# A hybrid decoder step: decode products in five heads, mixed rows loaded one group ahead, weighted rows turned in the last quarter

## Chip, core and metric

The kernel runs on one core of a Trainium2 chip. The metric is device time in microseconds. Before the change three runs gave 1744.0, 1746.33 and 1751.34 us, median 1746.33.

## The reference

One step of a hybrid decoder layer for a prompt of T = 1024 tokens and eight sample tokens, side by side as NT = 1032 columns, at model width 1024, in f32:

```python
h = rmsnorm(x, norm1_w)
q_r, f_r, i_r, g_r, z, xbc_r, dt_r = split(h @ w_in)
o_a = rmsnorm(hgrn2(silu(q_r), 1 - f, i_r, log(f)), hgrn_norm_w) * silu(g_r)      # 8 heads of 128
y   = rmsnorm((ssd(conv(xbc_r), dt) + D * X) * silu(z), ssm_norm_w)               # 16 heads of 64
x   = x + concat(o_a, y) @ w_out                                                   # 2048 -> 1024
gate, val = split(rmsnorm(x, norm2_w) @ w_up)                                      # 2 x 2816
x   = x + (silu(conv3(gate)) * val) @ w_down
y_out = rmsnorm(x, final_norm_w)
```

The prompt starts from zero states; the sample tokens update given states (one 128 x 128 matrix for each HGRN head and token, one 64 x 128 matrix for each SSM head and token), which are outputs too.

## The kernel before

Activations lie transposed: features on the 128 partitions, the 1032 columns along the free axis. Every large product is three f32r products, a high and a low part of each factor without low times low (`hh,wh`, `hl,wh`, `hh,wl`). ACT casts the high part (`split` and `split_in`, L199 and L1135), DVE subtracts for the low part (L201, L1136).

The input projection is a list of jobs of 128 output rows each (`z`, `xbc`, then `f q v sg` for each head). A stream of recurrence work is woven into it: `drive` runs a generator that yields weights, and after each yield lets PE do the share of matmul steps of the jobs that the weight stands for. `after(n, work)` runs work n steps later; `spread` runs the pieces of a generator n steps apart. So the order on every engine follows from the program's order and the yields.

The eight HGRN heads run in this weave, some 62 us each, beside the jobs of the next head. `head(h, t)` makes the values `vt`, decays `tt` and the intra-chunk products `a` in levels: `f`, `q`, `k`, `v` are scaled by `tt` (L980, L981, copies L983, L984), then short matmuls fill `a` at 128*64, 128*32 and 128*16. Then come the sample tokens' product `od` (from the states `Sh`, loaded by SP, updated by DVE at L959 and POOL at L958 and L960), the products `kv`, the running state `SS` (L1072, L1074), and the output `o`, normed and gated into `sg`. The head's `rstd` goes by DRAM (`hr_d`) to a broadcast `sq`; `scale_out` multiplies `sg` by it (L1121) and stores it as a row of `mix_d`, the mixed rows, from which the output projection reads.

The SSM decode has eight steps (two groups g, four steps i). `ssm_decode` runs in the z jobs, `decode_beside` beside a head: `load` (L690 to L693: state `Sd`, rows `Bb` and `Cb`), `front` (DVE `Bb`, ACT scaling of `Sd`, DVE sum, store, POOL products) and `back` (DVE reductions, L710, L711). Before, z jobs hold steps 0 and 1 of group 0, and heads 1 to 6 hold one step each. `load` is issued behind the state's store of the same head, `front` behind `od`'s copy, `back` behind the copy of its turned rows (L1081). Behind the last step of a group come `decode_gate` and, 80 steps later, `decode_norm` (L735 to L737, L730), which stores the sample columns of four mixed rows (L731). Rows 12 to 15 are complete only behind the second norm, which before stands in head 7.

The output projection runs in groups of four mixed rows. `mix_load(r0)` loads, casts and splits rows 8 to 11 beside head 6's end, and rows 12 to 15 beside head 7. The first group's results are copied out of PSUM by ACT (L1177).

SP issues nearly all DMAs, in order: one that waits holds up those behind it. Weights (`ws`) are loaded two jobs ahead.

At the end the down projection's last two groups of rows run by quarters of the columns, in the order 3, 0, 1, 2. For each quarter eight results are added to `x` (L1567), and each 128 columns are transposed (`fin`, L1574), squared and summed by ACT (L1576), rooted, and scaled by `rstd` and the final norm's weights (`fw`), then stored (L1588).

## Time and profile before

| what | us |
|---|---|
| median of three runs | 1746.33 |
| the profiled execution | 1747.35 |
| its span in the trace | 1745.6 |
| busy: PE, DVE, ACT, POOL | 1704.6, 1094.0, 782.0, 487.7 |

The trace has every instruction's start and duration; times are from the span's start. A row of the timeline has the start, the duration, engine, line, operation, the tiles out<-in, the shape, and in brackets how long the engine stood idle before it and what ended that. "issue" there means that the profile shows nothing that the engine waited for. `SPq` rows are the DMAs that SP issues. A window's DMA line gives the busy share of the 16 DMA engines in tenths, in 40 equal slices; `q8 instruction` are packets of instructions that are being fetched.

### The profile page before, as it was taken

What the parts mean: (1) busy time and instruction counts of PE and PEld (TensorE: products, weight loads), DVE (VectorE), ACT (ScalarE), POOL (GpSimd) and SP (SyncE); (2) the same over time, 40 slices, a digit from 0 to 9 for tenths busy, and PEclk for the clock granted to TensorE, in tenths of its full rate; (3) what the DMA queues carried; (4) which work ended last, traced back from release to release, by engine and by line L of the source; (5) the groups of instructions that cost most, each with busy time, mean ns of one, the idle gap of its engine ahead of it and who ended that gap; (6) DMA issues with size and microseconds to landing.
All of it is one profiled execution on the core that took longest, in us unless ns stands there. A gap on an engine that the chain in (4) does not pass through costs nothing. (4 is left out here: it accounts for less than half of the span.)

```text
span 1745.6 us, 38507 instructions
## 1 busy us (share of the span) xinstructions
PE 1704.6 (98%) x16119; PEld 1657.3 (95%) x16119; DVE 1094.0 (63%) x1979; ACT 782.0 (45%) x1427; POOL 487.7 (28%) x501
## 2 busy tenths in 40 slices
PE   7999999999999999999999989999999999999998
PEld 7999999899989999999999989999999999999997
DVE  6668666555754655567746688666767667444545
ACT  7677685344445444445333464333334434111114
POOL 2102131110210211111122266666666664000002
PEclk9999999999999999999999999999999999999999
DMA  5354334533442443345437722222222226422212
GB/s 165 73 123 123 92 91 146 157 90 101 137 127 64 137 123 99 112 141 155 138 125 244 239 81 78 82 96 74 74 73 81 79 97 214 154 71 79 94 61 98
DMA packets 250036, 200.22 MB, mean 115 GB/s; under 512 B 47972, under 2 KB 221526, under 8 KB 249846
## 3 DMA queue, kind: packets, MB, share of 16 engines
q1 hardware_dynamic: 249574, 197.67, 37.4%
q8 instruction: 126, 2.06, 0.5%
q14 instruction: 48, 0.39, 0.1%
q0 software_dynamic: 288, 0.10, 0.0%
HBM read 155.16 MB, written 46.95 MB: 116 GB/s over the span
## 5 line engine op out<-in xcount | busy, mean ns | idle before, releaser
L93 PE MATMUL mm<-hl,wh 128*128 128x344 f32 x1248 | 405.2, 325 | 0.0
L93 PE MATMUL mm<-hh,wh 128*128 128x344 f32 x1248 | 404.9, 325 | 0.0
L93 PE MATMUL mm<-hh,wl 128*128 128x344 f32 x1248 | 402.0, 322 | 0.0
L93 PEld LDWEIGHTS mm<-hl,wh 128*128 128x128 f32 x1248 | 235.3, 189 | 4.8 <-issue 4.1
L93 PEld LDWEIGHTS mm<-hh,wh 128*128 128x128 f32 x1248 | 235.3, 189 | 4.0 <-issue 3.4
L93 PEld LDWEIGHTS mm<-hh,wl 128*128 128x128 f32 x1248 | 235.4, 189 | 1.4 <-issue 1.2
L199 ACT CAST wh<-ws 128x1024 fp32r<-128x1024 f32 x96 | 100.6, 1048 | 260.7 <-PE dn L93 134.8
L93 PE MATMUL ub<-uh,wh 128*128 128x258 f32 x704 | 200.1, 284 | 3.8 <-DVE fext L1432 2.7
L93 PE MATMUL ub<-ul,wh 128*128 128x258 f32 x704 | 199.5, 283 | 0.0
L93 PE MATMUL ub<-uh,wl 128*128 128x258 f32 x704 | 199.4, 283 | 0.0
L93 PE MATMUL dn<-ah,wh 128*128 128x256 f32 (+1 forms) x640 | 181.2, 283 | 2.0 <-DVE x L1549 2.0
L93 PE MATMUL dn<-al,wh 128*128 128x256 f32 (+1 forms) x640 | 180.6, 282 | 0.0
L93 PE MATMUL dn<-ah,wl 128*128 128x256 f32 (+1 forms) x640 | 180.1, 281 | 0.0
L201 DVE TENSOR_TENSOR wl<-ws,wh 128x1024 fp32r<-128x1024 f32 x88 | 109.7, 1247 | 93.3 <-ACT wh L199 92.6
L93 PE MATMUL mm<-mh,wh 128*128 128x258 f32 x512 | 146.5, 286 | 4.1 <-DVE x L1179 4.0
L93 PE MATMUL ua<-uh,wh 128*128 128x258 f32 x528 | 149.5, 283 | 0.8 <-DVE val L1444 0.4
L93 PE MATMUL ua<-ul,wh 128*128 128x258 f32 x528 | 149.2, 282 | 0.0
L93 PE MATMUL ua<-uh,wl 128*128 128x258 f32 x528 | 148.4, 281 | 0.0
L93 PE MATMUL mm<-ml,wh 128*128 128x258 f32 x512 | 145.3, 284 | 0.6 <-DVE ml L1136 0.6
L93 PE MATMUL mm<-mh,wl 128*128 128x258 f32 x512 | 144.9, 283 | 0.0
L93 PEld LDWEIGHTS ub<-uh,wh 128*128 128x128 f32 x704 | 133.6, 190 | 4.4 <-DVE fext L1432 2.9
L1382 DVE TENSOR_TENSOR wl<-wt,wh 128x512 fp32r<-128x512 f32 x88 | 89.4, 1035 | 74.2 <-ACT wh L1381 74.2
(373 smaller groups left out, 3987.4 us busy)
## 6 DMA issues: line engine op xcount, KB each, us to landing
ws<-in_w_in_dram SPq DMA_DIRECT2D x52, 512.0 KB
ws<-in_w_up_dram SPq DMA_DIRECT2D x44, 512.0 KB
ws<-in_w_out_dram SPq DMA_DIRECT2D x24, 512.0 KB
act_d<-val SPq DMA_DIRECT2D x22, 516.0 KB
al<-act_d SPq DMA_DIRECT2D x22, 516.0 KB
ws<-in_w_down_dram SPq DMA_DIRECT2D x22, 512.0 KB
ml<-mix_d SPq DMA_DIRECT2D x48, 172.0 KB
csb<-cs_d SPq DMA_DIRECT2D x32, 256.0 KB
```

The lines of the kernel that those rows point to most:

```text
L93: PE.matmul(out, lhsT, rhs, start=start, stop=stop)
L199: A.copy(wh[:, :n], ws[:, :n])
L201: V.tensor_tensor(wl[:, :n], ws[:, :n], wh[:, :n].bitcast(F32), op=ALU.subtract)
L1382: V.tensor_tensor(lo[:, cs], sums[name], hi[:, cs].bitcast(F32), op=ALU.subtract)
```

## The change

1. `ssm_decode` runs three steps of group 0 in the z jobs in place of two; heads 1 to 5 hold the other five, head 6 none. So the norm of group 0 moves from head 3 to head 2, that of group 1 from head 7 to head 6.
2. In a head, the decode's `load` waits for the last `od` matmul, `front` stands behind `od`'s turned rows, `back` behind the head's `rstd`. `scale_out` of heads 0 to 6 moves to the next head, behind its `odr` copy.
3. `mix_ahead(12)` issues the twelve loads of rows 12 to 15 right behind those of rows 8 to 11; casts and splits follow in pieces, six steps apart.
4. The last quarter (`last_quarter`) weights the rows before they are turned (ACT, `fx`), squares and sums them untransposed (ACT `fq`, DVE `fa`), turns them between the products, gets the sums for both blocks by products with ones (`fs`), and scales at the end. The weights come as a column (`nf`) by one more load at the start.
5. The yield before the state's store in `ssd` goes from 1.0 to 3.0.

```diff
+    vec(2, "nf", final_norm_w.rearrange("(a b) -> a b", b=P))
...
         def load(behind):
-            with tc.issue_after(behind.ins):
-                SP.dma_start(d8(Sd), state_ssm[0, :, 2 * j:2 * j + 2].rearrange("b h p n -> (h p) b n"))
+            first_ = SP.dma_start(d8(Sd), state_ssm[0, :, 2 * j:2 * j + 2].rearrange("b h p n -> (h p) b n"))
+            tc.add_manual_dep(first_.ins, behind.ins.name,
+                              mybir.DependencyInfo(mybir.DependencyClass.Sync, mybir.DependencyReason.DATA))
+            with tc.issue_after(first_.ins):
                 SP.dma_start(Bb, bc_d[2 * g].rearrange("b n -> (b n)").unsqueeze(0).to_broadcast([P, T]))
...
-                if g and i % 2 == 0:
-                    ssm_decode(0, i // 2)
+                if g and i < 3:
+                    ssm_decode(0, i)
...
-        yield 1.0
+        yield 3.0
         ssm_state_out(g)
...
-        step_ = decode_beside((h + 1) // 4, (h + 1) % 4) if 1 <= h <= 6 else None
+        step_ = decode_beside((h + 2) // 4, (h + 2) % 4) if 1 <= h <= 5 else None
...
-        if step_:
-            step_[0](kept_)
...
-            mm(ops[32 * g:32 * g + 32, :P], qb[:, b, :], Sds[b // 4][:, b % 4, :], start=(b < 4), stop=(b >= 4))
+            oded = PE.matmul(ops[32 * g:32 * g + 32, :P], qb[:, b, :], Sds[b // 4][:, b % 4, :], start=(b < 4), stop=(b >= 4))
+        if step_:
+            step_[0](oded)
...
-        held = V.tensor_copy(odr, ops[:, :P])
-        if step_:
-            step_[1](held, turned_)
+        copied = V.tensor_copy(odr, ops[:, :P])
+        if unscaled:
+            unscaled.pop()(copied)
...
-        A.activation(od[:, 1, :], dps[:, :ND], AF.Square)
+        turned_ = A.activation(od[:, 1, :], dps[:, :ND], AF.Square)
+        if step_:
+            step_[1](held, turned_)
...
+        held = rstd_of(nt[:, 0:256], nt[:, 256:512], ps[:, :256], P)
+        if step_:
+            step_[2](held)
...
         after(16, spread_rstd)
-        after(48, scale_out)
+        if h < H - 1:
+            unscaled.append(scale_out)
+        else:
+            after(48, scale_out)
...
+    def mix_ahead(r0):
+        hi = [tl("hT", "mh", F32R) for _ in range(4)]
+        lo = [tl("hT", "ml", F32R) for _ in range(4)]
+        for cs in chunks:
+            for k in range(4):
+                fetch(lo[k][:, cs].bitcast(F32), mix_d[r0 + k, :, cs])
...
+                    split_in(hi[k], lo[k], cs)
...
+                if r0 == 8:
+                    ahead.append(mix_ahead(12))
+            if (r0, m) == (8, 2):
+                spread(ahead[0], 6)
+            elif (r0, m) == (12, 0):
+                for _ in ahead[0]:
+                    pass
...
+    def last_quarter(c):
...
+        for m in range(KT):
+            ps = down(lambda k: wd[k], nk, slice(m * P, (m + 1) * P), acts, c)
+            turned({4: (0, 1), 5: (2, 3), 6: (4, 5), 7: (6,)}.get(m, ()))
...
+            added = V.tensor_tensor(x_, x_, ps, op=ALU.add)
...
+            A.activation(xs[m], x_, AF.Copy, scale=col("nf", m))
...
+                A.activation(q_[-1], x_, AF.Square)
...
+            mm(sums[:, b:b + 1], acc_[:, blk[b]], ones[:, 0:1])
...
+        A.activation(r[:, 0:2], sums[:, 0:2], AF.Sqrt, bias=epsc, scale=1.0 / DM)
+        V.reciprocal(r[:, 2:4], r[:, 0:2])
...
     for c in (3, 0, 1, 2):
+        if c == 2:
+            last_quarter(c)
+            break
```

What that does to the order of instructions, at three places. First SP's queue in head 5, from the stores of the updated HGRN states to the store of the decode's state; line numbers of the changed kernel are a few higher. Before:

```order
L1122 DMA mix_d<-sg_6974 128x1032
L961 DMA out_dram<-Sh_7906 128x4x128
L961 DMA out_dram<-Sh_7914 128x4x128
L690 DMA Sd_7882<-in_state_ssm_dram 128x8x128
L691 DMA Bb_7883<-bc_d 128x1024
L693 DMA Cb_7884<-bc_d 128x512
L693 DMA Cb_7885<-bc_d 128x512
L196 DMA ws_8526<-in_w_in_dram 128x8x128
L182 DMA Sh_8685<-in_state_hgrn_dram 128x4x128
```

And after the change, the same head:

```order
L966 DMA out_dram<-Sh_7940 128x4x128
L966 DMA out_dram<-Sh_7948 128x4x128
L197 DMA ws_8560<-in_w_in_dram 128x8x128
L183 DMA Sh_8718<-in_state_hgrn_dram 128x4x128
L690 DMA Sd_7916<-in_state_ssm_dram 128x8x128
L694 DMA Bb_7917<-bc_d 128x1024
L696 DMA Cb_7918<-bc_d 128x512
L696 DMA Cb_7919<-bc_d 128x512
L1132 DMA mix_d<-sg_7008 128x1032
L183 DMA Sh_8726<-in_state_hgrn_dram 128x4x128
```

The decode's four loads now stand behind a weight's load and one of the next head's state loads, and the previous head's mixed row is stored behind them.

Second, DVE in head 7, from the values' product to the second scaling (`v` and `q` in this order are tiles that are used again under their first names; the last number of a row is its shape). Before:

```order
L1009 TENSOR_TENSOR v_9181<-q_8961,f_8715 128x1024
L1121 TENSOR_TENSOR sg_8532<-sg_8532,sq_9331 128x512
L986 TENSOR_TENSOR tt_9472<-f_8715 128x512
L1121 TENSOR_TENSOR sg_8532<-sg_8532,sq_9343 128x512
L201 TENSOR_TENSOR wl_9478<-ws_9476,wh_9477 128x1024
L1136 TENSOR_TENSOR ml_9489<-ml_9489,mh_9485 128x344 x2
L986 TENSOR_TENSOR tt_9473<-tt_9472 128x256
L735 SCALAR_TENSOR_TENSOR dg_9319<-dgs_9545,dg_9319 128x8
L980 TENSOR_TENSOR k_8952<-k_8952,f_8715 128x512
L736 SCALAR_TENSOR_TENSOR dg_9319<-dg_9319 128x8
```

After:

```order
L1012 TENSOR_TENSOR v_9207<-q_8998,f_8744 128x1024
L989 TENSOR_TENSOR tt_9491<-f_8744 128x512
L989 TENSOR_TENSOR tt_9492<-tt_9491 128x256
L989 TENSOR_TENSOR tt_9492<-tt_9492 128x128
L202 TENSOR_TENSOR wl_9497<-ws_9495,wh_9496 128x1024
L1149 TENSOR_TENSOR ml_9508<-ml_9508,mh_9504 128x344 x2
L1019 TENSOR_TENSOR amc_9493<-a_1091_9592,eyec 128x256
L989 TENSOR_TENSOR tt_9492<-tt_9492 128x64
L1149 TENSOR_TENSOR ml_9549<-ml_9549,mh_9545 128x344
L983 TENSOR_TENSOR k_8989<-k_8989,f_8744 128x512
L984 TENSOR_TENSOR v_9207<-v_9207,f_8744 128x512
```

The rows `sg` and `dg` are gone from here, and `ml_9549`, the first split of rows 12 to 15, stands ahead of `k`.

Third, ACT at the same place after the change; `x` is the eviction of the output projection's PSUM banks, `mh_9545` to `mh_9548` are the casts of rows 12 to 15:

```order
L1214 COPY x_1087_9565<-mm_9567 128x258
L1148 CAST mh_9545<-ml_9549 128x344
L1148 CAST mh_9546<-ml_9550 128x344
L1148 CAST mh_9547<-ml_9551 128x344
L1148 CAST mh_9548<-ml_9552 128x344
L1148 CAST mh_9545<-ml_9549 128x344
L1148 CAST mh_9546<-ml_9550 128x344
L1214 COPY x_1087_9565<-mm_9581 128x258
L1148 CAST mh_9547<-ml_9551 128x344
L986 COPY f_8744<-k_8989 128x256x2
```

Between the first two evictions stand six casts, where the table load and root of `dg` stood before, and a seventh ahead of the copy of `f`.

More of the change, by code (lines that the diff above doesn't have):

```diff
@@ L736, in rstd_of @@
         V.scalar_tensor_tensor(tmp, tmp, -0.5 / n, dst, op0=ALU.mult, op1=ALU.mult)
-        V.scalar_tensor_tensor(dst, tmp, 1.5, dst, op0=ALU.add, op1=ALU.mult)
+        return V.scalar_tensor_tensor(dst, tmp, 1.5, dst, op0=ALU.add, op1=ALU.mult)
     gr_d = dram.tile([2, 4, 256], F32, name="gr_d")
@@ L933, in head_in @@
         return t
+    unscaled = []
     def head(h, t):
         f, k, q, v, sg = (t[n] for n in ("f", "k", "q", "v", "sg"))
-        step_ = decode_beside((h + 1) // 4, (h + 1) % 4) if 1 <= h <= 6 else None
+        step_ = decode_beside((h + 2) // 4, (h + 2) % 4) if 1 <= h <= 5 else None
         dps = bank("vd", "nx")
@@ L960, in head @@
             G.tensor_tensor(Sd, Sd, vb, op=ALU.add)
-            kept_ = SP.dma_start(hgrn_sample[0, bs, h].rearrange("b k v -> k b v"), d4(Sd))
+            SP.dma_start(hgrn_sample[0, bs, h].rearrange("b k v -> k b v"), d4(Sd))
             Sds.append(d4(Sd))
-        if step_:
-            step_[0](kept_)
         hb = [slice(0, 512), slice(512, T)]
@@ L1043, in head @@
             A.copy(am[b:b + 32, :, b + 32:b + 64], c32(ps[:, :256])[b:b + 32])
-        turned_ = A.copy(am[0:64, :, 64:P], p6[0:64, :].rearrange("p (c t) -> p c t", t=64))
+        A.copy(am[0:64, :, 64:P], p6[0:64, :].rearrange("p (c t) -> p c t", t=64))
         ops = bank("od", "nx")
@@ L1081, in head @@
         held = V.tensor_copy(od[:, 0, :], dps[:, :ND])
-        A.activation(od[:, 1, :], dps[:, :ND], AF.Square)
+        turned_ = A.activation(od[:, 1, :], dps[:, :ND], AF.Square)
+        if step_:
+            step_[1](held, turned_)
         yield 3.2
-        if step_:
-            step_[2](held)
         for hf in range(2):
@@ L1107, in head @@
         nt = half("nt")
-        rstd_of(nt[:, 0:256], nt[:, 256:512], ps[:, :256], P)
+        held = rstd_of(nt[:, 0:256], nt[:, 256:512], ps[:, :256], P)
+        if step_:
+            step_[2](held)
         SP.dma_start(hr_d[h], nt[::32, 0:256])
@@ L1117, in spread_rstd, with scale_out @@
                 fetch(sq[hf], hr_d[h, 2 * hf:2 * hf + 2].rearrange("a t -> (a t)").unsqueeze(0).to_broadcast([P, 512]))
-        def scale_out():
+        def scale_out(behind=None):
             for hf in range(2):
-                V.tensor_tensor(sg[:, hb[hf]], sg[:, hb[hf]], sq[hf], op=ALU.mult)
+                with ExitStack() as order_:
+                    if behind is not None:
+                        order_.enter_context(tc.issue_after(behind.ins))
+                    V.tensor_tensor(sg[:, hb[hf]], sg[:, hb[hf]], sq[hf], op=ALU.mult)
             SP.dma_start(mix_d[h], sg[:, :NT])
         after(16, spread_rstd)
-        after(48, scale_out)
+        if h < H - 1:
+            unscaled.append(scale_out)
+        else:
+            after(48, scale_out)
     def split(src, hi, lo):
@@ L1145, in mix_load, with pieces @@
         return hi, lo
+    def mix_ahead(r0):
[4 more added lines that the diff above has]
+                fetch(lo[k][:, cs].bitcast(F32), mix_d[r0 + k, :, cs])
+        def pieces():
+            for cs in chunks:
+                for k in range(4):
+                    split_in(hi[k], lo[k], cs)
+                    yield
+        mixes[r0] = hi, lo
+        return pieces()
+    ahead = []
     mixes = {}
@@ L1562, in hybrid_layer, with turned, summed @@
         wd.append((hi, lo))
+    def last_quarter(c):
+        cs = quarters[c]
+        acc_ = tl("us", "fa")[:, :256]
+        tb = [[bank("fin"), bank("fin")] for _ in range(2)]
+        xs, q_ = [], [acc_]
+        def turned(ms):
+            for m in ms:
+                for b in range(2):
+                    PE.transpose(tb[b][m // 4][:, blk[m % 4]], xs[m][:, blk[b]], ident)
+        def summed():
+            return V.tensor_tensor(acc_, acc_, q_[-1], op=ALU.add)
+        for m in range(KT):
+            ps = down(lambda k: wd[k], nk, slice(m * P, (m + 1) * P), acts, c)
+            turned({4: (0, 1), 5: (2, 3), 6: (4, 5), 7: (6,)}.get(m, ()))
+            x_ = xT[m][:, cs]
+            if 1 < m < KT - 1:
+                summed()
+            added = V.tensor_tensor(x_, x_, ps, op=ALU.add)
+            if m == KT - 1:
+                with tc.issue_after(added.ins):
+                    summed()
+            xs.append(tl("us", "fx")[:, :256])
+            A.activation(xs[m], x_, AF.Copy, scale=col("nf", m))
+            if m:
+                q_.append(tl("us", "fq")[:, :256])
+            if m < KT - 1:
+                A.activation(q_[-1], x_, AF.Square)
+            else:
+                V.tensor_tensor(q_[-1], x_, x_, op=ALU.mult)
+        summed()
+        turned((KT - 1,))
+        sums = psmm.tile([P, 512], F32, tag="mm", name=nm("fs"))
+        for b in range(2):
+            mm(sums[:, b:b + 1], acc_[:, blk[b]], ones[:, 0:1])
+        r = keep.tile([P, 4], F32, tag="ss", bufs=4, name=nm("fss"))
+        A.activation(r[:, 0:2], sums[:, 0:2], AF.Sqrt, bias=epsc, scale=1.0 / DM)
+        V.reciprocal(r[:, 2:4], r[:, 0:2])
+        for b in range(2):
+            for i in range(2):
+                ot, t0 = tl("t", "ot"), cs.start + b * P
+                if i:
+                    A.activation(ot, tb[b][i], AF.Copy, scale=r[:, 2 + b:3 + b])
+                else:
+                    V.tensor_scalar(ot, tb[b][i], r[:, 2 + b:3 + b], None, op0=ALU.mult)
+                SP.dma_start(y_prompt[0, t0:t0 + P, i * 512:(i + 1) * 512], ot)
     for c in (3, 0, 1, 2):
+        if c == 2:
+            last_quarter(c)
+            break
         cs = quarters[c]
@@ L1581, in hybrid_layer @@
                 ds = slice(i * 512, (i + 1) * 512)
-                if i and c != 2:
+                if i:
                     A.activation(ot[i][:n], tb[i][:n, :], AF.Copy, scale=ss[:n, 3:4])
```

## The prediction

> **What bounds the kernel now.** I read the page first, then the list of what the engines waited for, then the stretches in which TensorE (PE) stood still.

> ```profile
> span 1745.6 us, 38507 instructions
> PE 1704.6 (98%) x16119; PEld 1657.3 (95%) x16119; DVE 1094.0 (63%) x1979; ACT 782.0 (45%) x1427; POOL 487.7 (28%) x501
> ```

> PE is busy for 1704.6 of 1745.6 us. The order in which PE runs its instructions is the same after the change as before it, except in the last quarter of the down projection. So the change can only take from the 41 us in which PE stands still, or add to them. The waits of PE:

> ```profile
> engine line waited for: us in total, times, longest us
> PE a L93 <- issue: 5.2, 3, 2.5
> PE sT L636 <- DVE S L611: 2.3, 1, 2.3
> PE a L93 <- DVE q L981: 2.3, 1, 2.3
> PE mm L93 <- DVE ml L1136: 0.6, 1, 0.6
> ```

> The rows left out, at the start and behind the output projection, stand before or behind all edits but one POOL load and the tail. Within reach are the two larger of the three "issue" waits, the two waits of head 7 (2.3 and 0.6), sT (2.3), and the stretch after the last matmul.

> **1. Decode loads behind the od product.** The "issue" waits, with the DMA engines around two of them (40 slices of a window of 8 us, then of 6 us):

> ```profile
> 522.25 0.29 PE L93 MATMUL a<-v,k 128*16 128x16 f32 x16 [2.49 <-issue]
> 649.51 0.21 PE L93 MATMUL a<-v,k 128*16 128x16 f32 x2 [1.92 <-issue]
> ...
> DMA  9995855789898899899999998755332100000000
> q8 instruction: 1, 0.02, 0.7%
> ```
> ```profile
> DMA  9999999998998999999799999999997431100000
> q8 instruction: 1, 0.02, 1.0%
> ```

> In windows 515 to 523 and 644 to 650 no engine holds PE up: it waits in the middle of short matmuls, two instructions each, of 16 columns. In both windows one packet of instructions is fetched while the DMA engines are nine tenths busy, and PE goes on soon after the traffic has drained. That traffic is the decode's: state, B and C rows, and a weight tile. In a third window the fetch falls where the DMA engines are idle, and there is no wait:

> ```profile
> DMA  0000000000090000000000000269999999999998
> q8 instruction: 1, 0.02, 2.7%
> ```

> This one is 639 to 641.5, whose end is the first of the decode's traffic in that head. After the change this traffic starts when the head's od product is through; here is when that was, in the same head:

> ```profile
> 658.01 0.65 PE L93 MATMUL od<-Sh,qb 128*32 128x128 f32 x16
> 677.04 0.39 PE L93 MATMUL o<-q,SS 128*128 128x128 f32 x2
> ```

> So it moves from 640 to about 659, behind all the short matmuls, among long ones, where an instruction lasts longer and a late fetch has more time. 2.49 + 1.92 = 4.4 us can go; the third (5.2 − 4.4 = 0.8) is in head 0, which has no such decode. Bounds: 0 (the wait is not the fetch's, or reappears) to −4.4. I take **−3.8**, nearer the full price, because both stalls end with the traffic and the quiet fetch had none.

> [...]

> What the step costs: it changes where the decode's work stands on DVE and ACT.

> ```profile
> 661.26 1.22 DVE L702 TENSOR_TENSOR Sd<-Sd,Bb 128x1024 f32<-128x1024 f32 x1
> 672.00 0.34 DVE L1074 SCALAR_TENSOR_TENSOR SS<-SS,tt,kv 128x128 f32<-128x128 f32 x1
> 674.08 1.22 DVE L201 TENSOR_TENSOR wl<-ws,wh 128x1024 fp32r<-128x1024 f32 x1 [1.66 <-ACT wh L199]
> ...
> 658.77 2.45 ACT L701 ACTIVATE Sd<-Sd,ddb 128x128 f32<-128x128 f32 x8
> 669.63 0.18 ACT L1082 ACTIVATE od<-odp 128x8 f32<-128x8 f32 x1 [1.81 <-DVE od L1081]
> ```

> Bb, Sd and wl now stand among the SS updates, which the o product reads one by one; the two reductions leave that place. The scalings on ACT end at 669.8 + 2.45 = 672.3, Sd at 673.5; wl keeps its 674.08 (it waits for a weight's cast, which waits for PE), and the last SS comes behind it, 674.08 + 1.2 + 0.3 = 675.6. The last o<-q,SS runs at 677.04: 1.4 us to spare, so **0**; if the loads (2 MB from 659, the scalings wait for them from 669.8) or ACT are later than that, the excess falls on PE in each of five heads. The stores of the previous head's weighted rows, and their two DVE products, come half a head later than before and are read only by the output projection. The loads of weights behind the waiting SP have a tile of lead.

> **2. Head 6 without decode, one more decode product in z.** What leaves head 7, and what stood around it:

> ```profile
> 810.88 1.23 DVE L1009 TENSOR_TENSOR v<-q,f 128x1024 f32<-128x1024 f32 x1 [0.59 <-PE vtp L945]
> 812.09 0.69 DVE L1121 TENSOR_TENSOR sg<-sg,sq 128x512 f32<-128x512 f32 x1
> 815.03 0.94 DVE L1136 TENSOR_TENSOR ml<-ml,mh 128x344 fp32r<-128x344 f32 x2
> 818.78 1.00 DVE L736 SCALAR_TENSOR_TENSOR dg<-dg 128x8 f32<-128x8 f32 x1
> 822.97 0.68 DVE L981 TENSOR_TENSOR q<-v,tt 128x512 f32<-128x512 f32 x1
> ...
> 815.60 0.39 PE L93 MATMUL mm<-ml,wh 128*128 128x258 f32 x1 [0.63 <-DVE ml L1136]
> 823.80 1.09 PE L93 MATMUL a<-q,f 128*32 128x32 f32 x64 [2.33 <-DVE q L981]
> ...
> 690.95 1.22 DVE L1009 TENSOR_TENSOR v<-q,f 128x1024 f32<-128x1024 f32 x1
> 698.23 1.80 DVE L981 TENSOR_TENSOR q<-v,tt 128x512 f32<-128x512 f32 x1
> ```

> The norm of the decode's second half (dg, L735 to L737) and the previous head's two sg products (0.6 each) leave DVE's row between v and q. Head 5 shows the row without dg, with POOL at work beside it as in head 7: from v to the end of q 700.03 − 690.95 = 9.1 us. For head 7 I take off the two sg (1.2), and add wl (1.2, which in head 5 lay ahead of v) and three splits of mixed rows (ml, 0.94 for two, so 0.43 apart: 1.3): 10.4, so q is through at 810.88 + 10.4 = 821.3. PE, without its 0.63 (the split ml is ahead by the sg's 1.2), comes to it at 823.80 − 2.33 − 0.63 = 820.84. 0.4 or so remains of 2.33: **−2.5** for both waits, between 0 and −2.96.

> The dg row is long because POOL works beside it; the same form took 0.17 in head 4:

> ```profile
> 679.68 0.17 DVE L735 SCALAR_TENSOR_TENSOR od<-dms,od 128x8 f32<-128x8 f32 x1 [0.83 <-ACT od L734]
> ```

> [...]

> The added decode in z (two of Bb, Sd, reduce at 0.7, eight scalings, two POOL products) lies at a place where DVE stood idle for 4.2 us at a time:

> ```profile
> 328.28 1.22 DVE L201 TENSOR_TENSOR wl<-ws,wh 128x1024 fp32r<-128x1024 f32 x1 [4.20 <-ACT wh L199]
> ```

> I cost it at **0**; uncovered it would be its DVE share, some 4 us. The yield before the state's store (1.0 to 3.0) changes no place in PE's order, so the 2.34 at sT stays: **0**.

> **3. Rows 12 to 15 loaded ahead.** Twelve loads of 172 KB, which SP issued in 6.51 us from 823.69, behind a store that waits for dg, now stand behind those of rows 8 to 11, the last two behind the Sh stores:

> ```profile
> 818.34 3.60 SPq L961 DMA_DIRECT2D out_dram<-Sh  x2
> 823.69 6.51 SPq L182 DMA_DIRECT2D ml<-mix_d  x12
> ...
> DMA packets 4530, 4.76 MB, mean 198 GB/s; under 512 B 843, under 2 KB 3887, under 8 KB 4527
> ```

> The last row is for 808 to 832. Their casts and splits now stand ahead of the copies and products of head 7, six casts ahead of one that empties a PSUM bank. If those 4.76 MB are through by 824.5, at 288 GB/s, the splits are done before PE needs the third product near 828: **0**, with about 1 us to spare. At the 198 GB/s of this row the last would land at 832.

> **4. The last quarter.** Before:

> ```profile
> 1731.17 0.69 ACT L1583 ACTIVATE ot<-fin,fss 128x512 f32<-128x512 f32 x1 [0.23 <-DVE fss L1579]
> 1741.05 1.41 DVE L1586 SCALAR_TENSOR_TENSOR ot<-fin,fss,fw 128x512 f32<-128x512 f32 x2
> 1739.73 3.08 SPq L1588 DMA_DIRECT2D out_dram<-ot  x4
> L1196 ACT ACTIVATE n2sq<-x 128x258 f32<-128x258 f32 x28 | 11.4, 416 | 12.3 <-DVE x L1179 12.3
> ```

> The sixteen transposes now go between the products, and the squares too. But ACT gets 15 operations of 256 columns from 1731.2 on (0.42 each by the last row, about 0.35 from one to the next), 5.3 us, beside four of the quarter before at up to 0.69, 2.8 us: its last weighted row is ready near 1739.3. Then two sums (0.7), the product with ones, root and reciprocal (1.0), and two scalings on each of DVE and ACT (1.4): 1742.4 against 1741.05 + 1.41 = 1742.46, and the four stores leave together where before two were on their way. **0**, between −0.7 and +0.7.

> **The sum.** −3.8 − 2.5 + 0 + 0 = −6.3, and I add 1 for new waits, one or two of the size of the 0.6 above, since the work of five heads and twelve loads change places: −5.3. The profiled execution took 1747.35 us (span 1745.6 and 1.75 around it), 1.0 above the median: 1747.35 − 5.3 − 1.0 = **1741.0**.

> **The rivals.**
> - *The issue waits stay*, or a fetch is late elsewhere, as under the mixed rows' loads. For: the third issue wait, 0.8 without decode traffic. Against: the quiet window. Only head 7 gains: 1746.3 − 2.5 + 1 = 1745. Chance 0.18.
> - *Slower: the twelve loads hold up head 7.* If the DMA moves less than 288 GB/s between 808 and 824.5, ACT and DVE stand at a cast whose rows have not landed, with the copies of head 7 behind it. At 198 GB/s that is 7.5 us in place of the 2.5 gained, and the bank that is not emptied stops PE: 1746.3 − 3.8 + 7.5 = 1750. For: the mean of the row; SP waits 3.60 us at the Sh stores. Against: 335 to 405 GB/s in single slices. Chance 0.14.
> - *The SS updates come late in five heads*, from 1.4 us on; at 1 us beyond it 1741 + 5 = 1746. Chance 0.1.
> [...]
> - *More than all terms*, as where the tail gains or a stall that I left standing goes with them: −4.4 − 2.96 − 0.7 gives 1738, a little more gives 1736. Chance 0.1.

> **How the numbers follow.** The forecast (1738.5 to 1744) has 0.48. The range 1736 to 1751 takes in the rivals at 1745, 1746 and 1750 and leaves out the far tails. 0.5% is 8.7 us, about what a measurement of this kernel can tell from no change (its three runs lie 7.3 apart): faster, below 1737.6, 0.1; slower, above 1755.1, 0.06; the rest 0.84.

> **What would show it.** Right: no "issue" wait at the 16-column matmuls of heads 2 and 4; a<-q,f of head 7 waits under 1 us; the od product is followed by the decode's loads and PE's o product waits for no SS. Wrong: an "issue" wait at another place, ACT waiting for ml between 816 and 826, PE waiting for a PSUM bank or for SS, or a last store that is issued more than 6 us after the last down product.

## The result, and the profile after

The changed kernel takes **1750.85 us** (median of 15 runs, 1745.51 to 1753.08), against 1746.33 before: ratio 1.0023, interval 1.0013 to 1.0032. It is slower by some 4 us; the forecast was 5.3 faster. The profiled execution took 1749.07 us, its span is 1747.4. What PE waited for in it, the rows that the change concerns:

```profile
PE mm L93 <- ACT x L1214: 5.2, 2, 3.6
PE sT L637 <- DVE S L612: 2.2, 1, 2.2
PE a L93 <- issue: 2.2, 3, 1.1
PE fin L1609 <- ACT fx L1625: 0.8, 3, 0.3
```

The "issue" waits fell from 5.2 to 2.2, and one of those that are left stands in head 7. The waits of head 7 for DVE (2.3 and 0.6) are gone, and PE waits there 5.2 us for ACT to empty a PSUM bank (`x<-mm`), a row that the kernel before did not have. The stretches tell where the time went: from head 0 to head 7, from head 7 to the up projection, and from the down projection to the end. The columns are the window, its length, PE's busy time and instructions, its granted clock, the DMA share and rate. Before:

```profile
372.60:809.70 437.10, 431.90 (x5731) 1.00 0.40 117
809.70:1022.80 213.10, 205.63 (x2079) 0.99 0.59 185
1472.10:1745.60 273.50, 263.43 (x2208) 0.99 0.30 101
```

And after:

```profile
372.80:804.30 431.50, 430.37 (x5732) 1.00 0.38 114
804.30:1022.40 218.10, 207.55 (x2078) 0.98 0.57 181
1471.20:1747.40 276.20, 265.31 (x2211) 0.99 0.29 101
```

The heads gain 5.6 us, head 7 with the output projection loses 5.0, the tail loses 2.7. These two executions lie 1.8 us apart, where the medians lie 4.5 apart: the one of before took 1.0 us more than its median, the one of the changed kernel 1.8 less. A loss ahead of head 0, which this pair does not show, comes up in the last section. Head 7 in detail, the changed kernel's ACT, SP, POOL, DVE and PE:

```profile
821.39 0.48 ACT L1148 CAST mh<-ml 128x344 fp32r<-128x344 f32 x1 [3.55 <-DMA ml<-mix_d]
824.57 0.48 ACT L1148 CAST mh<-ml 128x344 fp32r<-128x344 f32 x1 [2.71 <-DMA ml<-mix_d]
825.48 0.36 ACT L1214 COPY x<-mm 128x258 f32<-128x258 f32 x1
...
816.78 0.39 SPq L966 DMA_DIRECT2D out_dram<-Sh  x1
817.21 0.50 SPq L183 DMA_DIRECT2D ml<-mix_d  x1
821.46 0.39 SPq L966 DMA_DIRECT2D out_dram<-Sh  x1
821.89 0.51 SPq L183 DMA_DIRECT2D ml<-mix_d  x1
...
816.71 3.11 POOL L963 TENSOR_TENSOR vb<-vb,k 128x512 f32<-128x512 f32 x1
819.90 1.53 POOL L965 TENSOR_TENSOR Sh<-Sh,vb 128x512 f32<-128x512 f32 x1
...
820.19 1.78 DVE L983 TENSOR_TENSOR f<-f,tt 128x512 f32<-128x512 f32 x1
...
825.89 0.39 PE L93 MATMUL mm<-mh,wh 128*128 128x258 f32 x1 [3.60 <-ACT x L1214]
```

Read from below: PE stands until 825.89 for the copy of 825.48. ACT reaches that copy only behind the cast of 824.57, whose rows SP asked for at 821.89. DVE did not hold ACT up: its `f`, which ACT copies between that cast and the copy of 825.48, was ready at 820.19 + 1.78 = 821.97. SP was not late because the DMA engines were full, but because the load stands behind the store of `Sh`, which waits for POOL's sum: 819.90 + 1.53 = 821.43. From 808 to 824.5 the DMA engines moved 176 GB/s, less than the 288 of the prediction, but they stood idle for a part of it (busy tenths, 40 slices):

```profile
DMA  9999745878699989610000069994000000099897
```

Behind that comes something the list of waits does not show:

```profile
823.36:826.77 3.41, 0.88 (x7) 1.00 0.68 211
826.77:830.18 3.41, 2.36 (x131) 0.50 0.05 15
830.18:833.60 3.42, 3.42 (x17) 0.50 1.00 320
```

In a stretch of 3.41 us PE is busy for 0.88 us, and in the two stretches behind it the granted clock is 0.50. The matmuls of 258 columns take 0.42 us there in place of 0.28.

### The profile page after: what moved, and what is told of

It reads as the page before. It is cut to its first block, busy times and chain, and to the rows that moved or that the text cites. A ratio compares the mean times of both kernels' runs of the same rounds, so it can differ in the third digit from the quotient of the medians.

```text
span 1747.4 us, 38541 instructions
## 1 busy us (share of the span) xinstructions
PE 1706.1 (98%) x16123; PEld 1656.8 (95%) x16123; DVE 1091.5 (62%) x1984; ACT 788.2 (45%) x1438; POOL 486.1 (28%) x502
## 5 line engine op out<-in xcount | busy, mean ns | idle before, releaser
L93 PE MATMUL mm<-hl,wh 128*128 128x344 f32 x1248 | 405.1, 325 | 0.0
L93 PE MATMUL mm<-hh,wh 128*128 128x344 f32 x1248 | 404.6, 325 | 0.0
L93 PE MATMUL mm<-hh,wl 128*128 128x344 f32 x1248 | 401.7, 322 | 0.0
L93 PEld LDWEIGHTS mm<-hl,wh 128*128 128x128 f32 x1248 | 235.1, 188 | 4.8 <-issue 4.1
L93 PEld LDWEIGHTS mm<-hh,wh 128*128 128x128 f32 x1248 | 235.0, 188 | 3.1 <-issue 2.5
L93 PEld LDWEIGHTS mm<-hh,wl 128*128 128x128 f32 x1248 | 235.2, 188 | 1.4 <-issue 1.2
L93 PE MATMUL ub<-uh,wh 128*128 128x258 f32 x704 | 200.1, 284 | 3.3 <-DVE fext L1469 2.7
L93 PE MATMUL ub<-ul,wh 128*128 128x258 f32 x704 | 199.4, 283 | 0.0
L93 PE MATMUL ub<-uh,wl 128*128 128x258 f32 x704 | 199.1, 283 | 0.0
L93 PE MATMUL dn<-ah,wh 128*128 128x256 f32 (+1 forms) x640 | 181.5, 284 | 2.3 <-DVE x L1586 2.1
L93 PE MATMUL dn<-ah,wl 128*128 128x256 f32 (+1 forms) x640 | 180.6, 282 | 0.0
L93 PE MATMUL dn<-al,wh 128*128 128x256 f32 (+1 forms) x640 | 180.5, 282 | 0.0
L202 DVE TENSOR_TENSOR wl<-ws,wh 128x1024 fp32r<-128x1024 f32 x88 | 114.9, 1306 | 83.6 <-ACT wh L200 83.3
L93 PE MATMUL mm<-mh,wh 128*128 128x258 f32 x512 | 147.5, 288 | 9.3 <-ACT x L1214 5.2
L93 PE MATMUL ua<-uh,wh 128*128 128x258 f32 x528 | 149.6, 283 | 1.3 <-DVE val L1481 1.3
L93 PE MATMUL ua<-uh,wl 128*128 128x258 f32 x528 | 149.4, 283 | 0.0
L93 PE MATMUL ua<-ul,wh 128*128 128x258 f32 x528 | 148.7, 282 | 0.0
L93 PE MATMUL mm<-ml,wh 128*128 128x258 f32 x512 | 146.1, 285 | 0.2 <-DVE ml L1149 0.2
L93 PE MATMUL mm<-mh,wl 128*128 128x258 f32 x512 | 145.7, 285 | 0.0
L93 PEld LDWEIGHTS ub<-uh,wh 128*128 128x128 f32 x704 | 133.5, 190 | 3.9 <-DVE fext L1469 2.9
```

Of the source, the lines that this page charges most:

```text
L93: PE.matmul(out, lhsT, rhs, start=start, stop=stop)
L202: V.tensor_tensor(wl[:, :n], ws[:, :n], wh[:, :n].bitcast(F32), op=ALU.subtract)
```

## The experiments

Each is the changed kernel with one edit, unless said otherwise; each ratio is to the kernel before. The theory that they test: **head 7** loses its time because casts of rows that have not landed stand in ACT's order ahead of the copies that empty PSUM (theory 1). The rival: **the last quarter** is the loss (theory 2).

**1. Casts behind head 7** (`casts_late`). Casts and splits of rows 12 to 15 come behind the `od` product's copies, the loads stay ahead.

```diff
-            if (r0, m) == (8, 2):
-                spread(ahead[0], 6)
-            elif (r0, m) == (12, 0):
+            if (r0, m) == (12, 0):
...
-                    split_in(hi[k], lo[k], cs)
+                    x_ = lo[k][:, cs].bitcast(F32)
+                    with tc.issue_after(passed[0].ins):
+                        A.copy(hi[k][:, cs], x_)
+                    with tc.issue_after(passed[1].ins):
+                        V.tensor_tensor(lo[k][:, cs], x_, hi[k][:, cs].bitcast(F32), op=ALU.subtract)
```

`passed` holds the head's last copy into `am` (ACT) and its copy of `odr` (DVE).

> The changed kernel, with the casts and splits of rows 12 to 15 put behind the last copy into am (ACT) and the odr copy (DVE) of head 7; the loads stay ahead. Theory 1 (ACT stands at a cast whose rows have not landed, with the copies that empty PSUM behind it, and PE then runs at half clock for two windows): the waits of PE for ACT x in head 7 (1.61 and 3.60 us) and most of the half clock go, 5 to 6 us less than the changed kernel, so about 1745. Theory 2 (the last quarter is what makes the kernel slower): no difference, 1750 to 1751.

Measured: 1744.45 us, ratio 0.9978 (0.9966 to 0.9991), 4.5 to 4.9 thousandths below the changed kernel (1.0023, and 1.0027 in run 5), so 8 us, more than the 5 to 6 expected. From head 7 to the up projection its trace takes 209.7 us, where the changed kernel took 218.1. ACT at the same place:

```profile
821.17 0.63 ACT L987 COPY k<-f 128x512 f32<-128x512 f32 x1 [2.31 <-DVE f L984]
821.70 0.36 ACT L1218 COPY x<-mm 128x258 f32<-128x258 f32 x1
834.74 1.62 ACT L1174 CAST mh<-ml 128x344 fp32r<-128x344 f32 x4
```

No copy waits for a cast, PE's list has no row with `ACT x`, and the half clock in head 7 is gone (1.00 from 822 to 834). The edit moves DVE's splits along with ACT's casts; that it is ACT's order which counts rests on the rows of head 7 above. Theory 1 stands, and with this edit alone the kernel is faster than before.

**2. The two stores from POOL** (`stores_pool`).

```diff
-            SP.dma_start(hgrn_sample[0, bs, h].rearrange("b k v -> k b v"), d4(Sd))
+            (G if h == H - 1 else SP).dma_start(hgrn_sample[0, bs, h].rearrange("b k v -> k b v"), d4(Sd))
```

> The changed kernel, with the two stores of head 7's updated HGRN states issued by POOL in place of SP, so that the last two of the twelve loads do not stand behind them in SP's queue. Theory 1 with SP's order as the reason that the rows land late: the second wait (3.60 us) falls under 1 us, the first (1.61) stays, 3 to 4 us less than the changed kernel, 1747 to 1748. If the DMA engines' rate were the reason (theory 1 as the prediction had it): the rows land as late as before, 1750 to 1751.

Measured: 1747.94 us, ratio 0.9999 (0.9986 to 1.0013). SP's last six loads of the twelve now leave in one go, and the wait for ACT falls from 5.2 to 2.7:

```profile
812.77 3.54 SPq L183 DMA_DIRECT2D ml<-mix_d  x6
```
```profile
PE mm L93 <- ACT x L1214: 2.7, 2, 2.0
PE a L93 <- issue: 1.7, 1, 1.7
```

The second wait is 0.65 us, the first stays at 2.0, as expected from SP's order as the reason. The DMA rate is not it: the last load is issued by 816.3, not at 821.89. The ratio lies 4 us below the changed kernel's 1.0023, as forecast.

**3. The last quarter as before** (`tail_back`).

```diff
     for c in (3, 0, 1, 2):
-        if c == 2:
-            last_quarter(c)
-            break
...
-                if i:
+                if i and c != 2:
```

> The changed kernel, with the last quarter as it was before. Theory 1: only what the traces show for the tail, 1.2 us less, 1749.5. Theory 2: all of the loss, 4 to 4.5 us less, 1746.5.

Measured: 1747.52 us, ratio 0.9998 (0.9985 to 1.0011), by the ratios 4.4 us less than the changed kernel: the number of theory 2. The traces give less. From the down projection to the end its profile takes

```profile
1471.50:1745.00 273.50, 263.46 (x2208) 0.99 0.30 101
```

273.5 us, as before, where the changed kernel took 276.2. Of these 2.7 us, 1.1 lie ahead of the last quarter, where the edit changes nothing. From the first product of the last quarter to the end, the five profiles with the new quarter take 17.3 to 17.7 us, the eight with the old one 15.5 to 15.8: it costs some 1.8 us. Between `casts_late` and `casts_tail` below the same edit moved the ratio by 0.0008 only, 1.4 us. The profile's head 7 still waits 5.3 us for ACT. So both theories hold a part, and the last quarter is the smaller one; the rest of this run's 4.4 us is about what its interval leaves open (2.3 us to either side).

**4. The decode's loads where they were** (`loads_back`).

```diff
+            with tc.issue_after(behind.ins):
+                SP.dma_start(d8(Sd), state_ssm[0, :, 2 * j:2 * j + 2].rearrange("b h p n -> (h p) b n"))
...
+            kept_ = SP.dma_start(hgrn_sample[0, bs, h].rearrange("b k v -> k b v"), d4(Sd))
...
+        if step_:
+            step_[0](kept_)
...
-        if step_:
-            step_[0](oded)
```

> The changed kernel, with the decode's loads issued behind the stores of the HGRN states again (front and back stay where the change put them). If the late loads are what took away the issue waits of heads 2 and 4: the waits return in those two heads, with half clock behind one of them, 4 to 6.5 us more than the changed kernel, 1755 to 1757. If the place of the fetch moved by chance: no such waits, 1750 to 1751.

Measured: 1752.93 us, ratio 1.0027 (1.0014 to 1.004), between the two forecasts and not told apart from the changed kernel. The trace shows a wait of 1.66 us in head 4 again and 0.25 in head 2, with no half clock behind either.

**5. The changed kernel again** (`changed_again`), without an edit.

> The changed kernel itself, as the control of this group and for a second profile of it. If the half clock falls on windows of 3.41 us whose place against the program is a matter of chance, the profile shows the same waits of PE as the first one (ACT x in head 7 about 5 us, sT about 2.3 us), and the half-clock windows behind other ones of them; 1.002 times the kernel before. If a stall alone decides the clock, the windows stand at the same places as in the first profile.

Measured: 1751.56 us, ratio 1.0027 (1.0015 to 1.0038). The waits return, and the half clock stands elsewhere: behind sT too (0.78 on the mean from 314.5 to 317.9), where the first profile had none.

```profile
PE mm L93 <- ACT x L1214: 4.6, 2, 2.9
PE sT L637 <- DVE S L612: 2.9, 1, 2.9
```
```profile
821.61:825.02 3.41, 3.41 (x57) 0.50 0.46 123
831.85:835.26 3.41, 3.41 (x123) 0.50 0.16 43
```

**6. Both losses taken out** (`casts_tail`): edits 1 and 3 together.

> The casts of rows 12 to 15 behind head 7's od and the last quarter as before: what is left of the change are the decode edits, the loads of rows 12 to 15 ahead and the moved stores. Theory (head 7's stall and the tail are the two losses, 5 to 7 and 2.3 us): 8 us less than the changed kernel, 4 to 6 less than the kernel before. Rival (the decode edits gain nothing, and what casts_late gained was chance): within 2 us of the kernel before.

Measured: 1741.93 us, ratio 0.997 (0.9957 to 0.9982): 5 us faster than before, 9 to 10 faster than the changed kernel. What is left of the change gains about what the prediction's sum had (5.3); how the gain divides among its edits, this run does not show.

**7. As 6, the decode's loads where they were** (`casts_tail_loads`): edits 1, 3 and 4.

> As casts_tail, with the decode's loads behind the stores of the HGRN states again. If the later loads bring the gain in the heads: 2 to 6 us more than casts_tail, with issue waits in the 16-column matmuls of head 2 or head 4. If not: within 1 us of casts_tail.

Measured: 1744.01 us, ratio 0.9978 (0.9968 to 0.9989). The intervals overlap; the medians lie 2 us apart, the ratios 1.4, so neither forecast is settled by them. Head 4 waits 1.84 us at "issue" again, head 2 does not.

**8. As 6, without the wait at sT** (`casts_tail_st`). The first decode product of the z jobs begins in its job's last chunk, and its B rows are scaled behind the last S update.

```diff
-                if g and i < 3:
+                if g and 0 < i < 3:
                     ssm_decode(0, i)
...
+                if g and i == 0 and c == NCH - 1:
+                    ssm_decode(0, 0)
...
-            V.tensor_tensor(Sn, Sn, st, op=ALU.add)
+            last_S[:] = [V.tensor_tensor(Sn, Sn, st, op=ALU.add)]
...
-            V.tensor_tensor(d4(Bb), d4(Bb), cb(xdd[:, 0, bs]), op=ALU.mult)
+            with tc.issue_after(last_S[0].ins):
+                V.tensor_tensor(d4(Bb), d4(Bb), cb(xdd[:, 0, bs]), op=ALU.mult)
```

> As casts_tail, with the first decode product of the z jobs begun in the job's last chunk and its B rows scaled behind the last S update on DVE: takes away the wait that the yield of 3.0 did not. sT's 2.2 to 2.8 us and, in some executions, a window of half clock (1.7 us) go: 2 to 4 us less than casts_tail. If another product or the decode's end takes its place: no difference.

Measured: 1737.79 us, ratio 0.9944 (0.9932 to 0.9956), the fastest of all, 4.1 us below `casts_tail` by the medians and 4.5 by the ratios. In the changed kernel DVE stands at B rows that have not landed, with S behind them:

```profile
314.15 0.69 DVE L671 TENSOR_TENSOR Bb<-Bb,xdd 128x512 f32<-128x512 f32 x1 [0.91 <-DMA Bb<-bc_d]
314.76 0.68 DVE L612 TENSOR_TENSOR S<-S,st 128x512 f32<-128x512 f32 x1
```

Here S goes first, and sT no longer waits:

```profile
311.65 0.67 DVE L612 TENSOR_TENSOR S<-S,st 128x512 f32<-128x512 f32 x1
313.39 0.69 DVE L674 TENSOR_TENSOR Bb<-Bb,xdd 128x512 f32<-128x512 f32 x1 [1.07 <-DMA Bb<-bc_d]
```

**9 and 10. The kernel before, twice** (`before_2`, `before_3`), without an edit, for the spread of its profile.

> The kernel before, for a second profile. If the issue wait of 2.5 us in head 2 belongs to the kernel, it is there again, with the 1.9 in head 4; if it hangs on when a fetch meets the decode's traffic, one of them may be missing. The half-clock windows stand at other places than 523, 823 and 1042 if their place is chance.

> The kernel before, for a third profile, with the same two questions as before_2: which of the issue waits of heads 2 and 4 return, and behind which waits the half-clock windows stand.

Measured: 1750.28 and 1745.07 us, one run each. The first row is of `before_2`, the second of `before_3`:

```profile
PE a L93 <- issue: 5.6, 4, 2.2
```
```profile
PE a L93 <- issue: 4.0, 4, 1.8
```

The waits return at 523 and 649 with other lengths (1.14 and 2.19, then 0.79 and 0.73), and there is one more in head 5 (1.55, 1.77), which the first profile of before did not have. The wait at 523 has 2.49, 1.14 and 0.79 us in three executions of one program. The half clock begins at 825.06 and 1043.51 in the one, at 823.25 and 1038.29 in the other: behind the same waits of head 7 and of the up projection as in the first profile (823.37, 1041.82). Only the stretch in head 2 (523.00) does not return.

**11. Rows 12 to 15 loaded as before, the last quarter as before** (`mix_tail_back`): edit 3, and

```diff
-                if r0 == 8:
-                    ahead.append(mix_ahead(12))
-            if (r0, m) == (8, 2):
-                spread(ahead[0], 6)
-            elif (r0, m) == (12, 0):
-                for _ in ahead[0]:
-                    pass
```

> The changed kernel with rows 12 to 15 loaded, cast and split where the first job that reads them begins, as before, and the last quarter as before; the decode edits stay. If the early loads were worth something once the casts are out of the way: 2 us or more above casts_tail's ratio of 0.997, with waits for mixed rows in head 7. If they are worth nothing: the same ratio within 0.001.

Measured: 1747.61 us, ratio 1.0005 (0.9993 to 1.0017), against 0.997 for `casts_tail`: 6 us above it, as the first forecast had it. But the trace shows another reason than the worth of the early loads, the stall of head 7 once more:

```profile
823.38 1.00 ACT L1148 CAST mh<-ml 128x344 fp32r<-128x344 f32 x2 [2.54 <-DMA ml<-mix_d]
827.68 0.36 ACT L1207 COPY x<-mm 128x258 f32<-128x258 f32 x1
```
```profile
828.10 0.58 PE L93 MATMUL mm<-mh,wh 128*128 128x258 f32 x1 [3.94 <-ACT x L1207]
```

Without `mix_ahead` the loads are issued early all the same, one ahead of the two stores of `Sh`, one between and ten behind them, since the store that they waited for before (the norm's, now in head 6) no longer holds them; the casts follow. So the call that loads ahead is not needed for the stall. Nor is a waiting cast ahead of a copy enough: the kernel before has one too, and PE does not stand behind it.

```profile
826.30 0.88 ACT L1135 CAST mh<-ml 128x344 fp32r<-128x344 f32 x2 [4.09 <-DMA ml<-mix_d]
```

The copy behind it comes at 827.09. PE had waited for `q` until 823.80 and works on without a wait until past this copy. I take it that PE, once it no longer waits for DVE, needs the next empty bank sooner, so that the cast must be out of its way; no run isolates that. What early loads alone are worth, this run does not tell.

## Why the prediction was wrong, point by point

- **"The change can only take from the 41 us in which PE stands still": failed.** A term was left out, the clock. In the profile of before, three stretches of 3.41 us had the clock at 0.50 (a fourth comes at the end, when PE is done), each worth up to 1.7 us by my estimate, half its length; the page's line of tenths, which shows 9 throughout, hides them. In the changed kernel two such stretches follow the stall of head 7. PE's order is not quite unchanged either: four products of the decode's norms (`dgs`, 128x8) stand one head earlier; no wait stands at them.
- **Decode loads, −3.8: the mechanism is borne out, the size in part by luck.** The issue waits of the heads fell from 4.0 to 5.6 us in three profiles of before to 0.3 to 1.1 in two of the changed kernel, and the heads from 434.7 to 437.1 us to 431.5 and 430.8. But the profile that I read had the longest waits in heads 2 and 4 (4.4 us, against 3.3 and 1.5 in the other two), and the half-clock stretch in head 2 that the others lack. With the loads alone put back, these waits come to 1.9 and 1.8 us, nearly all in head 4, and the heads take 433.2 and 433.1 us; in the eight profiles with the late loads heads 2 and 4 have none. So the place of the loads is worth some 2 us in the traces. The medians don't tell 2 us apart, and which of the decode edits took away the rest in head 2 is open.
- **"The waits are the fetch's": argued there only from two windows, and the traces have more.** All 33 "issue" waits of PE in the thirteen profiles end 2.2 to 3.0 us after a packet of instructions begins to be fetched (2.5 and 2.4 us in heads 2 and 4 of before), though they are 0.2 to 2.5 us long; packets come some 14 us apart on the mean. In head 4 that packet begins when PE has started 6066 to 6073 of its matmuls in the eight profiles with the late loads, and 6081 to 6207 in the five with the early ones. So beside the decode's loads the fetch comes later in PE's work. But such a wait also comes up elsewhere: head 7 has an "issue" wait of 0.5 to 1.7 us in nine of the ten profiles with decode edits and in none of the three of before. The prediction named that as a sign of being wrong, and had 1 us in its sum for all new waits.
- **SS updates on time, 0: right** in most profiles; `mix_tail_back` and `casts_tail` show one wait of 0.8 and 0.4 us for SS in one head.
- **Head 7, −2.5: the waits for DVE went, as said**, and the step was swallowed by the next. With the casts out of the way (`casts_late`) the stretch takes 209.7 us in place of 213.1; a half-clock stretch, which stands there in all three profiles of before, is a part of these 3.4.
- **Rows 12 to 15 ahead, "0, with about 1 us to spare": this step failed.** The rival was named, with the wrong key. I had the landing of the rows hang on the DMA rate (288 GB/s), and had "the last two behind the Sh stores" in one half-sentence without a price. `stores_pool` shows that the stores are the key to the second wait, `casts_late` that ACT's order is the key to both. The rival's total, 1750, lies near the measured 1750.85 by luck: its price of 7.5 us in place of the 2.5 gained was too high (the stretch from head 7 on lost 5.0 in the first pair of profiles), and the losses of the last quarter and ahead of head 0 were not in it.
- **z product and yield, 0: right for the wait;** sT waits 2.2 to 3.0 us in every kernel but `casts_tail_st`. The clock behind that wait is another matter (last section).
- **The last quarter, 0 between −0.7 and +0.7: mis-sized.** It costs some 1.8 us (run 3). ACT's operations took 0.49 (weighted rows) and 0.40 (squares), a pair 0.71 from start to start, close to my 0.35 each. What I left out: eight transposes now stand ahead of the end of the last product on PE, so that its last matmul starts at 1737.05 where before it started at 1735.89, from a quarter that began 0.1 later; and the sums end on DVE 1.2 us behind the last weighted row:

```profile
1738.76 0.49 ACT L1625 ACTIVATE fx<-x,vcol 128x256 f32<-128x256 f32 x1
1739.55 0.88 DVE L1612 TENSOR_TENSOR fa<-fa,fq 128x256 f32<-128x256 f32 x2
1740.48 0.61 PE L93 MATMUL fs<-ones,fa 128*128 128x1 f32 x4 [0.73 <-DVE fa L1612]
1741.62 1.41 DVE L1646 TENSOR_SCALAR ot<-fin,fss 128x512 f32<-128x512 f32 x2
1742.38 1.79 SPq L1647 DMA_DIRECT2D out_dram<-ot  x4
```

The four stores leave from 1742.38 on, where before the first of four left at 1739.73 and the others followed; from the last product's last matmul to the end it takes 10.3 us in place of 9.7. The sign that I named, a last store more than 6 us behind the last product, tells nothing: it is 6.6 us in the kernel before and 6.7 after.

## What to carry to other kernels

ACT came to a copy that empties PSUM only behind two casts that had waited 3.55 and 2.71 us for their rows, and with the casts behind head 7's copies the kernel took 8 us less: pull the load ahead, not its consumer. SP issued the last of the moved loads at 821.89, behind a store that waited for POOL until 821.43; with the stores out of its queue it had issued them all by 816.3, and PE's second wait fell from 3.60 to 0.65 us: look at every store between the loads that are moved and ask what it waits for. And behind the wait of 3.60 us the clock was at 0.50 for 6.83 us, in a kernel whose mean is 0.996: count a wait of PE with the clock behind it, and read the granted clock by the stretch, not by the mean.

## What the runs showed of the hardware that I had not expected

```profile
311.37:314.78 3.41, 1.60 (x11) 1.00 1.00 332
314.78:318.20 3.42, 2.88 (x20) 1.00 0.24 67
```
```profile
819.95:823.37 3.42, 1.52 (x71) 1.00 0.35 98
823.37:826.78 3.41, 2.98 (x73) 0.50 0.57 131
```
```profile
310.95:314.36 3.41, 1.50 (x10) 1.00 1.02 342
314.36:317.77 3.41, 2.59 (x10) 0.50 0.18 49
317.77:321.19 3.42, 3.42 (x13) 0.50 0.31 91
```

And one with more work, in head 7 of `changed_again`, where most matmuls of the cell have 32 columns; behind it the clock was at 0.50 all the same:

```profile
818.20:821.61 3.41, 1.69 (x110) 1.00 0.10 32
```

With 1.60 us busy the next cell kept its clock, with 1.52 and 1.50 it did not. In the profiles of before and of the changed kernel, between 20 and 1730 us, the cells at full clock with 0.88, 0.93, 0.96 and 1.52 us busy were followed by half clock, and none with 1.60 or more was. A second cell stayed at half where the first was busy for 2.36 us (changed kernel), 2.59 (`mix_tail_back`) and 2.70 (`casts_tail`), not where it was busy for 2.98 or 3.41 (before). So the wait at sT, 2.3 us in the profile of before and 3.0 in `casts_tail`, had no half-clock cell behind it in the one and two in the other, by my estimate up to 1.7 us for each. The first cell began 0.75 us behind the span's start in the profile of before, 0.74 in the changed kernel's, 2.45 in `before_2`, 0.64 in `before_3` and 2.41 in `changed_again`. I take this place to be a part of the spread between runs of one program (8.2 us in the 15 runs of the kernel before); no run isolates it. In the profiles with the decode edits and a wait at sT, sT drew a half-clock cell in seven of nine, and in the three of before in none. Head 0 begins at 372.6 to 374.8 us in the five profiles without such a cell, at 375.1 to 377.3 in the seven with one, and at 371.5 in `casts_tail_st`, which has no wait there. This is the loss that the first pair of profiles does not show. Whether the change made such a cell likelier, or three draws were lucky, is left open.
